# One diffusion-transformer layer on one core: output-weight factors, split attention rows, head norm per pair, routing by four tiles

## The chip, the cores and the metric

One Trainium2 core runs the whole layer as one program. The metric is the device time of one execution in microseconds; "before" is the median of three runs. The engines are PE (matrix products), DVE (VectorE), ACT (ScalarE), POOL (GpSimd) and SP (SyncE, which issues most DMAs). Each engine takes its instructions strictly in order and meets the others at semaphores.

## The reference

The layer takes 2048 latent tokens and 256 context tokens of width 1024. After adaptive norm and one input projection, half of the columns go to attention (8 query heads of 64, 2 key/value heads), half to a short gated convolution in 8 groups of 64 channels. Each head's output is RMS-normalised with its own gain, both halves are joined and projected, and the result is added with a gate. A second adaptive norm feeds a mixture of experts: one of 4 groups, then two of its 8 experts, each a SwiGLU of inner width 768.

```python
def merge_out(a, cv, attn_g, conv_g, w_out):
    return concat([head_rms(a, attn_g, 8), head_rms(cv, conv_g, 8)], axis=-1) @ w_out

x_new = x + gt1 * merge_out(ax, convx, attn_out_g, conv_out_g, w_out)
hx2 = rms_norm(x_new, norm2_g) * (1 + sc2) + sh2
x_new = x_new + gt2 * hier_moe(hx2, ...)      # top 1 of 4 groups, top 2 of 8 experts
out = rms_norm(x_new, final_g)
```

Inputs and outputs are float32. The kernel reaches that accuracy from float16 products: an operand is stored as a float16 part and the float16 remainder ("hi" and "lo"), and three products (hi by hi, hi by lo, lo by hi) take the place of one.

## The kernel before

**Stages.** First (0 to 235 us of the profile) queries, keys and values are projected, normalised, rotated and stored. The attention stage follows, to 1417 us: 32 units (four blocks of 512 queries by 8 heads, `units`), each of nine steps of two key tiles. In a step PE makes scores (`scores`, L480), ACT exponentiates them twice, as float32 and as float16, DVE or POOL subtracts the one from the other (`rest`, L494: after the convolution every other step goes to POOL), and PE multiplies with the values (`values`, L503). The softmax needs each query's maximum beforehand: `max_piece` (L456) multiplies 128 queries with up to 512 keys into one of three PSUM banks `mxp`, and DVE reduces the bank to a column. The 2304 keys are four pieces of 512 and one of 256, so a unit has 20 pieces; they run about a unit ahead of the scores.

Between these steps PE is given fillers (`fillers`, L1016): first the convolution (`conv_gen`, up to 895 us), beside it the modulation and the output weights (`out_weights`, L673), then, from 895 us, the output projection of the first twelve token tiles (`out_gen`, L975). A tail from 1417 to 1545 us does the last four tiles and the remaining routing, and begins to load expert weights. The expert stage follows.

**What the change touches.** `finish_unit` (L520) ends a unit: copy from PSUM to `ob`, squares, sum, POOL's power -1/2, product `on`; after every odd head the pair is transposed through the PSUM bank `ms` (a tag with one bank, which the maxima, the logits and the routing use too), scaled by the gain column on ACT into `oT` and stored to the DRAM tensor `mixT` as float32. `load_mix` (L748) later loads a token tile of 8 x 128 columns, and `split_mix` (L760) multiplies the convolution half by gain and reciprocal root, then makes hi and lo of both halves: in the attention stage on DVE, in the tail with the casts on ACT. `last_mix` (L770) does the last head pair, which may arrive later. `proj` (L776) makes 48 products of 512 columns per tile into PSUM, `evict` adds the residual. `logits` (L825) transposes the row, makes the second norm and the 36 router logits; `route` (L846), after every second tile, picks groups and experts with some thirty small DVE instructions and two exponentials, counts slots with small products on PE and scatters the token entries to `lists` by indirect DMAs from POOL, one for each tile and choice.

**What sets the order.** The loop from L1099 writes a step's scores, maxima, values, one filler at a pace (`fill`, L1085) and the pieces of `finish_unit`; `go_on` (L962) advances logits and routing. From this text a planner at compile time lays out the order of each engine. It may move instructions past others of the same engine; what it lays out is then fixed.

Of the kernel before, what the change touches and what calls it, by code (L numbers as in the profile page):

```python
# [9 lines left out]
F32 = mybir.dt.float32  # L10
F32R = mybir.dt.float32r
F16 = mybir.dt.float16
# [47 lines left out]
def tile_block(ctx: ExitStack, tc: tile.TileContext, x, c, ctxt, c_ctx, w_mod, b_mod, norm1_g, w_in,  # L60
# [17 lines left out]
    mixT = dram.tile([KT, P, S], F32, name="mixT")  # L78
# [59 lines left out]
    eps_l = kvp.tile([P, 1], F32, name="eps_l")  # L138


    with ExitStack() as st:
# [281 lines left out]
        V.tensor_scalar(eps_l, pb, 1024.0, None, op0=OP.mult)  # L423
        vfv = vf.rearrange("p t (g d) -> p t g d", g=2)
# [7 lines left out]
    if True:  # L432
# [23 lines left out]
        def max_piece(u, j, i):  # L456
            h = u[1]
            o, n = PIECES[i]
            if j == 0 and i == 0:
                rowmax[u] = sm.tile([P, 4, len(PIECES)], F32, name="mx")  # L460
            p_ = pp.tile([P, 512], F32, name="mxp", bufs=3)
            T.matmul(p_[:, :n], q1[u][:, j * P:(j + 1) * P], k1T[:, h // 4, o:o + n], start=True, stop=True)  # L462
            V.tensor_reduce(rowmax[u][:, j, i:i + 1], p_[:, :n], axis=AX.X, op=OP.max)  # L463
# [56 lines left out]
        def finish_unit(u):  # L520
            cq, h = u
            ob = op_.tile([P, 4, HD + 1], F32, name="ob", bufs=2)
            A.copy(ob, oraw.pop(u))  # L523
            yield
            sq = op_.tile([P, 4, HD], F32, name="osq")
            A.activation(sq, ob[:, :, 0:HD], AF.Square)
            l1 = sm.tile([P, 4], F32, name="ol1")
            V.tensor_scalar(l1, ob[:, :, HD], eps_l, None, op0=OP.mult)
            l2 = sm.tile([P, 4], F32, name="ol2")
            V.scalar_tensor_tensor(l2, l1, EPS, l1, op0=OP.mult, op1=OP.mult)  # L530
            yield
            ss = sm.tile([P, 4], F32, name="oss")
            V.tensor_reduce(ss, sq, axis=AX.X, op=OP.add)
            var = sm.tile([P, 4], F32, name="ovar")
            V.scalar_tensor_tensor(var, ss, 1.0 / HD, l2, op0=OP.mult, op1=OP.add)
            r = sm.tile([P, 4], F32, name="orr")
            G.tensor_tensor(r, var, mhalf[:, :4], op=OP.pow)
            yield
            if h % 2 == 0:
                pair[cq] = op_.tile([P, 4, 2, HD], F32, name="on", bufs=2)  # L540
            on = pair[cq]
            V.tensor_mul(on[:, :, h % 2], ob[:, :, 0:HD], r[:, :, None].to_broadcast([P, 4, HD]))
            if h % 2:
                yield
                k = h // 2
# [3 lines left out]
                oT = op_.tile([P, QC], F32, name="oT", bufs=2)  # L549
# [8 lines left out]
        def conv_gen():  # L558
# [5 lines left out]
            def finish(ct, vb, gb, n, t0, lo):  # L564
                t1 = cp.tile([P, CH], F32, name="t1", bufs=2)
                V.tensor_scalar(t1[:, :n], vb[:, 0:n], cols[:, 32 + ct:33 + ct], None, op0=OP.mult)
# [3 lines left out]
                nc.sync.dma_start(mixT[4 + ct, :, t0 + lo:t0 + n], t1[:, lo:n])  # L570
# [102 lines left out]
        def out_weights():  # L673
            g1 = mp.tile([P, D], F32, name="g1")
# [12 lines left out]
            for q, (k, n) in enumerate(todo):  # L687
# [5 lines left out]
                A.activation(woh[:, k, cs], s_, AF.Copy, scale=WS)  # L693
                V.scalar_tensor_tensor(wol[:, k, cs], s_, WS, woh[:, k, cs], op0=OP.mult, op1=OP.subtract)
# [53 lines left out]
        def load_mix(bp, tt):  # L748
            ts = slice(tt * P, (tt + 1) * P)
            mf = bp.tile([P, KT, P], F32, name="mf")  # L750
            nc.sync.dma_start(mf[:, 4:8], mixT[4:8, :, ts].rearrange("k p s -> p k s"))
            n = ready[tt] + 1
            dm["sp"] = nc.sync.dma_start(mf[:, 0:n], mixT[0:n, :, ts].rearrange("k p s -> p k s"))
# [4 lines left out]
            return mf, rb, n  # L758

        def split_mix(bp, mf, rb, after_attn):  # L760
            for k in range(4):
                V.scalar_tensor_tensor(mf[:, 4 + k], mf[:, 4 + k], cols[:, 28 + k:29 + k], rb[:, k], op0=OP.mult, op1=OP.mult)
            mh = bp.tile([P, KT, P], F16, name="mh")
            ml = bp.tile([P, KT, P], F16, name="ml")
# [3 lines left out]
            return mh, ml  # L768

        def last_mix(mf, mh, ml, tt):  # L770
            if loads[tt][2] < 4:
                dm["sp"] = nc.sync.dma_start(mf[:, 3], mixT[3, :, tt * P:(tt + 1) * P])
            V.tensor_copy(mh[:, 3], mf[:, 3])
            V.tensor_sub(ml[:, 3], mf[:, 3], mh[:, 3])

        def proj(bp, mf, mh, ml, xt, tt, banks, eng):  # L776
# [4 lines left out]
            def part(po, n, ks):  # L781
                cs = slice(n * 512, (n + 1) * 512)
                for ko, k in enumerate(ks):
                    for i, (m_, w_) in enumerate(((mh, woh), (mh, wol), (ml, woh))):
# [825 lines left out]
```

## Time and profile before

| | |
|---|---|
| Runs | 2559.11, 2562.71, 2563.91 us; median 2562.71 |
| Profiled execution | 2567.82 us, of which the span 2566.0 |
| Granted clock, mean | 0.956 |
| PE | 2317.3 us, 90% of the span |
| DVE | 2013.4 us, 78% |
| ACT | 1684.5 us, 66% |
| POOL | 673.4 us, 26% |

The span runs from the first to the last instruction of the profiled execution. In a group of instructions a row gives line, engine, operation, output and inputs with shapes, the count, the busy time of all and the mean of one, and then the idle time of the engine just ahead of them with what ended it. A wait row reads "who, at which line, waited for whom: us in total, times, longest". The granted clock is the share of TensorE's full speed of 2.4 GHz that was granted, as a mean over the stretch; its lower level is 1.2 GHz.

### The profile page before, as it was taken

The page shows a single profiled execution, that of the slowest core. Times are in us where ns is not written, and L with a number is a line of the kernel's source. Part 1 is how long each engine was busy: PE and PEld are TensorE (multiplying, and loading weights), DVE is VectorE, ACT ScalarE, POOL GpSimd, SP SyncE. Part 2 cuts the span into 40 slices and gives each one's busy share as a digit, 9 for nine tenths or more (in the row PEclk, how much of TensorE's full clock was granted, in tenths as well). Part 3 has the DMA queues.
Part 4 walks back from the last instruction along what each step waited for, and adds up shares of the span by engine and source line. Part 5 has one row for each costly group of instructions (what it writes and reads, how often), then busy time and mean ns, then how long its engine had stood idle before and what let it go on. Part 6 is the DMA issues. An engine that isn't in the chain of part 4 may idle for free. (4 is left out here: it accounts for less than half of the span.)

```text
span 2566.0 us, 64760 instructions
## 1 busy us (share of the span) xinstructions
PE 2317.3 (90%) x26923; PEld 1784.0 (70%) x26923; DVE 2013.4 (78%) x3480; ACT 1684.5 (66%) x3177; POOL 673.4 (26%) x442
## 2 busy tenths in 40 slices
PE   7998988989999988979888949999999999999964
PEld 2555765666777745545455539999899989999953
DVE  4777789898777788888887747778788887888865
ACT  4764555666666765656556427777778886888853
POOL 1331124221222234444444231121111121111122
PEclk9998999999999989999999969999999999999987
DMA  8543133341111052112211768999999999999986
GB/s 310 201 122 89 58 124 103 101 130 52 49 34 51 30 112 78 48 62 69 69 51 50 251 209 301 319 331 332 329 360 355 358 355 339 342 351 356 349 310 242
DMA packets 230215, 499.25 MB, mean 195 GB/s; under 512 B 50465, under 2 KB 97949, under 8 KB 226846
## 3 DMA queue, kind: packets, MB, share of 16 engines
q1 hardware_dynamic: 192054, 429.41, 47.8%
q0 software_dynamic: 16032, 39.85, 6.2%
q10 hardware_dynamic: 21832, 25.82, 2.9%
q8 instruction: 212, 3.47, 0.5%
q14 instruction: 85, 0.70, 0.1%
HBM read 427.20 MB, written 67.90 MB: 193 GB/s over the span
## 5 line engine op out<-in xcount | busy, mean ns | idle before, releaser
L1194 DVE SCALAR_TENSOR_TENSOR wr<-raw,wr 128x1024 f16<-128x1024 f32 x576 | 684.1, 1219 | 111.7 <-ACT wr L1192 109.5
L1192 ACT ACTIVATE wr<-raw 128x1024 f16<-128x1024 f32 x576 | 587.4, 1055 | 79.8 <-DMA raw<-in_w_down_dram 23.8
L491 ACT ACTIVATE pf<-st 128x512 f32<-128x512 f32 x576 | 345.1, 599 | 283.9 <-PE st L490 225.4
L463 DVE TENSOR_REDUCE mx<-mxp 128x1 f32<-128x512 f32 (+1 forms) x640 | 392.5, 629 | 69.4 <-PE mxp L462 68.3
L498 POOL TENSOR_TENSOR pl<-pf,ph 128x1024 f16<-128x1024 f32 x125 | 273.4, 2187 | 621.8 <-PE o L516 274.3
L1345 PEld LDWEIGHTS <-wr 128*128 128x128 f16 x4032 | 396.8, 98 | 20.5 <-issue 17.5
L1346 PEld LDWEIGHTS <-wr 128*128 128x128 f16 x4032 | 396.3, 98 | 13.2 <-issue 8.6
L1344 PEld LDWEIGHTS <-wr 128*128 128x128 f16 x4032 | 396.4, 98 | 4.2 <-issue 0.9
L492 ACT ACTIVATE ph<-st 128x512 f16<-128x512 f32 x576 | 344.6, 598 | 0.0
L1344 PE MATMUL pu<-x,wr 128*128 128x152 f16 (+19 forms) x1536 | 295.8, 227 | 8.1 <-DVE sg L1361 7.7
L1344 PE MATMUL pg<-x,wr 128*128 128x152 f16 (+19 forms) x1536 | 295.0, 226 | 3.3 <-ACT sg L1359 2.9
L1346 PE MATMUL pg<-x,wr 128*128 128x152 f16 (+19 forms) x1536 | 294.5, 226 | 3.6 <-DVE wr L1194 3.5
L1345 PE MATMUL pu<-x,wr 128*128 128x152 f16 (+19 forms) x1536 | 295.6, 227 | 0.0
L1346 PE MATMUL pu<-x,wr 128*128 128x152 f16 (+19 forms) x1536 | 295.4, 227 | 0.0
L1345 PE MATMUL pg<-x,wr 128*128 128x152 f16 (+19 forms) x1536 | 294.6, 226 | 0.0
L615 PE MATMUL z<-h,cwh 128*128 128x256 f16 x1536 | 275.8, 275 | 9.9 <-DVE vb L623 6.4
L462 PE MATMUL mxp<-k1T,q 128*128 128x512 f16 (+1 forms) x640 | 231.5, 365 | 38.5 <-DVE mx L463 37.1
L516 PE MATMUL o<-vh,pl 128*128 128x65 f16 x2304 | 246.8, 196 | 7.1 <-DVE pl L500 4.6
L514 PE MATMUL o<-vh,ph 128*128 128x65 f16 x2304 | 247.7, 197 | 0.3 <-ACT ob L523 0.2
L515 PE MATMUL o<-vlo,ph 128*128 128x64 f16 x2304 | 247.4, 195 | 0.0
L489 PE MATMUL st<-q,k1T 128*128 128x512 f16 x576 | 222.2, 386 | 16.1 <-ACT ph L492 15.5
L514 PEld LDWEIGHTS <-ph 128*128 128x128 f16 x2304 | 218.0, 100 | 22.1 <-issue 6.6
(363 smaller groups left out, 5414.2 us busy)
## 6 DMA issues: line engine op xcount, KB each, us to landing
raw<-in_w_down_dram SPq DMA_DIRECT2D x64, 1536.0 KB
raw<-in_w_gate_dram SPq DMA_DIRECT2D x63, 1536.0 KB
raw<-in_w_up_dram SPq DMA_DIRECT2D x63, 1536.0 KB
xt<-in_x_dram SPq DMA_DIRECT2D x32, 512.0 KB
wmod<-in_w_mod_dram SPq DMA_DIRECT2D x64, 256.0 KB
h<-hs SPq DMA_DIRECT2D x16, 1024.0 KB
w<-in_w_mod_dram SPq DMA_DIRECT2D x16, 512.0 KB
hs<-h ACTq DMA_DIRECT2D x8, 1024.0 KB
```

The source lines that it names most:

```text
L463: V.tensor_reduce(rowmax[u][:, j, i:i + 1], p_[:, :n], axis=AX.X, op=OP.max)
L491: A.activation(pf[:, i], p_, AF.Exp)
L492: A.activation(ph[:, i], p_, AF.Exp)
L498: G.tensor_tensor(pl, pf, ph, op=OP.subtract)
L514: T.matmul(po[:, j], ph[:, i, js], vh1[:, k, g], start=f, stop=False, skip_group_check=True)
L515: T.matmul(po[:, j, 0:HD], ph[:, i, js], vlo[:, k, g], start=False, stop=False, skip_group_check=True)
L615: T.matmul(z, w_[:, k, cs], h[:, a_, k, :], start=(n == 0), stop=(n == 3 * KT - 1))
L1192: A.activation(w[:, 0, sl], t[:, sl], AF.Copy, scale=WS)
L1194: V.scalar_tensor_tensor(w[:, 1, sl], t[:, sl], WS, w[:, 0, sl], op0=OP.mult, op1=OP.subtract)
L1344: T.matmul(p_[:, :C], w_[:, 0, kk, cs], x[:, 0, k, :C], start=first, stop=False)
L1345: T.matmul(p_[:, :C], w_[:, 0, kk, cs], x[:, 1, k, :C], start=False, stop=False)
L1346: T.matmul(p_[:, :C], w_[:, 1, kk, cs], x[:, 0, k, :C], start=False, stop=last)
```

## The change

- The gains of both halves (attention and convolution) leave the rows and go into the output weights: `out_weights` scales by a column `wg` = gain x 256 instead of 256.
- `finish_unit` copies both heads of a pair into one tile and does squares, sums, root and product once per pair. The square of the softmax sums with its epsilon moves from two DVE instructions to one on ACT (`eps_q`). After the transpose ACT makes the hi part from PSUM, DVE the lo part, and two DMAs store them to `mixA`, laid out by token tile in pieces of 256 bytes.
- `load_mix` loads the convolution half as float32 and the attention half as the two parts, straight into the tile that `proj` reads. `split_mix` is left with one product of 512 columns, a cast on ACT and one subtraction, all for the convolution half; `last_mix` with a load.
- `route` handles four tiles at once for the first twelve tiles, two for the last four. Its tiles are twice as wide; a four-tile call makes eight scatters.
- The 256-key pieces of two query blocks share a bank and one reduction: 18 pieces per unit instead of 20.
- The first product of the convolution's three taps moves from DVE to ACT.

```diff
+            if h % 2:
+                sq = op_.tile([P, 8, HD], F32, name="osq")
+                A.activation(sq.rearrange("p (h j) d -> p h j d", h=2), ob[:, :, :, 0:HD], AF.Square)
+                A.activation(l2, ob.rearrange("p h j d -> p (h j) d")[:, :, HD], AF.Square, scale=eps_q)
...
+                V.tensor_reduce(ss, sq, axis=AX.X, op=OP.add)
+                V.scalar_tensor_tensor(var, ss, 1.0 / HD, l2, op0=OP.mult, op1=OP.add)
+                G.tensor_tensor(r, var, mhalf[:, :8], op=OP.pow)
+                V.tensor_tensor(on.rearrange("p j h d -> p h j d"), ob[:, :, :, 0:HD], ...)
...
-                A.activation(oT, tq, AF.Copy, scale=cols[:, 24 + k:25 + k])
-                nc.sync.dma_start(mixT[k, :, cq * QC:(cq + 1) * QC], oT)
+                A.copy(oT[:, 0], tq)
+                V.tensor_sub(oT[:, 1], tq, oT[:, 0])
+                for a in range(2):
+                    nc.sync.dma_start(mixA[cq * 4:(cq + 1) * 4, :, a, k].rearrange("j p s -> p j s"),
+                                      oT[:, a].rearrange("p (j s) -> p j s", j=4))
...
-                V.tensor_scalar(t1[:, :n], vb[:, 0:n], cols[:, 32 + ct:33 + ct], None, op0=OP.mult)
+                A.activation(t1[:, :n], vb[:, 0:n], AF.Copy, scale=cols[:, 32 + ct:33 + ct])
...
+            for a, j in enumerate(js):
+                T.matmul(p_[:, a * n:(a + 1) * n], q1[u][:, j * P:(j + 1) * P], k1T[:, h // 4, o:o + n], start=True, stop=True)
+            V.tensor_reduce(rowmax[u][:, js[0]:js[-1] + 1, i:i + 1], p_[:, :len(js) * n].rearrange("p (a n) -> p a n", a=len(js)),
+                            axis=AX.X, op=OP.max)
...
-            mf = bp.tile([P, KT, P], F32, name="mf")
-            nc.sync.dma_start(mf[:, 4:8], mixT[4:8, :, ts].rearrange("k p s -> p k s"))
-            n = ready[tt] + 1
-            dm["sp"] = nc.sync.dma_start(mf[:, 0:n], mixT[0:n, :, ts].rearrange("k p s -> p k s"))
+            mf = bp.tile([P, 4, P], F32, name="mf")
+            dm["sp"] = nc.sync.dma_start(mf, mixT[:, :, ts].rearrange("k p s -> p k s"))
...
+            m = bp.tile([P, 2, KT, P], F16, name="mh")
+            n = ready[tt] + 1
+            dm["sp"] = nc.sync.dma_start(m[:, :, 0:n], mixA[tt, :, :, 0:n])
...
-            for k in range(4):
-                V.scalar_tensor_tensor(mf[:, 4 + k], mf[:, 4 + k], cols[:, 28 + k:29 + k], rb[:, k], op0=OP.mult, op1=OP.mult)
-            for ks in (slice(4, 8), slice(0, 3)):
-                (A.copy if after_attn else V.tensor_copy)(mh[:, ks], mf[:, ks])
-                V.tensor_sub(ml[:, ks], mf[:, ks], mh[:, ks])
+            V.tensor_mul(mf, mf, rb)
+            A.copy(m[:, 0, 4:8], mf)
+            V.tensor_sub(m[:, 1, 4:8], mf, m[:, 0, 4:8])
...
-            V.tensor_copy(mh[:, 3], mf[:, 3])
-            V.tensor_sub(ml[:, 3], mf[:, 3], mh[:, 3])
...
+            n2 = 4 if tt < NT - 4 else 2
...
-            for i in range(4):
+            for i in range(2 * n2):
                 w_ = G.indirect_dma_start(out=lists[:, :], ...)
...
-                if tt % 2:
-                    after.append([route(tt - 1), None])
+                if tt % 2 and tt >= NT - 4:
+                    after.append([route(tt - 1, 2), None])
+                elif tt % 4 == 3:
+                    after.append([route(tt - 3, 4), None])
```

## Rows read from the trace of the kernel before

**Rows 1.** Windows by stage: from:to, length; busy PE, PEld, DVE, ACT, POOL; clock; DMA
```profile
390.00:642.00 252.00, 232.60 (x2677) 162.82 (x2676) 225.88 (x393) 160.47 (x336) 66.75 (x37) 0.98 0.31 96
642.00:895.00 253.00, 252.35 (x3072) 184.10 (x3070) 193.47 (x366) 172.35 (x353) 61.11 (x32) 1.00 0.12 39
895.00:1417.00 522.00, 450.44 (x4757) 274.00 (x4756) 427.27 (x797) 311.94 (x631) 231.13 (x128) 0.92 0.25 69
1545.00:2438.00 893.00, 872.97 (x12167) 827.61 (x12165) 734.34 (x974) 703.41 (x1196) 157.72 (x94) 1.00 0.99 343
```

**Rows 2.** PE's waits, 895 to 1417: us in total, times, longest
```profile
PE mxp L462 <- DVE mx L463: 35.0, 20, 4.7
PE st L489 <- ACT ph L492: 7.9, 19, 1.1
...
PE o L516 <- POOL pl L498: 2.4, 3, 1.0
```

**Rows 3.** DVE's waits, 895 to 1417, same columns
```profile
DVE mf L762 <- DMA mf<-mixT: 15.3, 6, 3.7
DVE h L820 <- POOL n2r L118: 12.9, 5, 5.4
DVE on L542 <- POOL orr L537: 10.8, 10, 2.6
```

**Rows 4.** DVE instruction groups, 895 to 1417: busy us, mean ns; idle before
```profile
L463 DVE TENSOR_REDUCE mx<-mxp 128x1 f32<-128x512 f32 x205 | 136.2, 681 | 16.2 <-PE mxp L462 15.8
...
L463 DVE TENSOR_REDUCE mx<-mxp 128x1 f32<-128x256 f32 x52 | 21.4, 412 | 5.5 <-PE mxp L462 5.5
L762 DVE SCALAR_TENSOR_TENSOR mf<-mf,cols,rb 128x128 f32<-128x128 f32 x56 | 21.2, 422 | 20.4 <-DMA mf<-mixT 15.3 <-DMA rb<-cvrs 3.1 <-issue 2.0
L542 DVE TENSOR_TENSOR on<-ob,orr 128x256 f32<-128x256 f32 x14 | 18.9, 1352 | 10.8 <-POOL orr L537 10.8
L767 DVE TENSOR_TENSOR ml<-mf,mh 128x512 f16<-128x512 f32 x13 | 15.5, 1195 | 0.0
...
L767 DVE TENSOR_TENSOR ml<-mf,mh 128x384 f16<-128x384 f32 x13 | 11.4, 879 | 0.0
L766 DVE CAST mh<-mf 128x512 f16<-128x512 f32 x12 | 10.6, 886 | 0.2 <-PE z L785 0.2
L773 DVE CAST mh<-mf 128x128 f16<-128x128 f32 x12 | 10.5, 877 | 0.0
L774 DVE TENSOR_TENSOR ml<-mf,mh 128x128 f16<-128x128 f32 x12 | 10.3, 862 | 0.0
L766 DVE CAST mh<-mf 128x384 f16<-128x384 f32 x12 | 7.5, 626 | 1.0 <-DMA mf<-mixT 1.0
L528 DVE TENSOR_SCALAR ol<-ob,eps_l 128x4 f32<-128x4 f32 x14 | 7.5, 534 | 0.0
...
L902 DVE TENSOR_TENSOR ee<-ee,pen 128x64 f32<-128x64 f32 x5 | 5.0, 990 | 2.1 <-ACT ee L861 2.1
...
L931 DVE TENSOR_TENSOR en<-en,m 128x2 f32<-128x2 f32 x5 | 0.8, 150 | 0.0
```

**Rows 5.** DVE instruction groups of the tail, 1417 to 1545
```profile
L767 DVE TENSOR_TENSOR ml<-mf,mh 128x512 f16<-128x512 f32 x3 | 2.1, 684 | 0.0
L767 DVE TENSOR_TENSOR ml<-mf,mh 128x384 f16<-128x384 f32 x3 | 1.7, 551 | 0.0
...
L773 DVE CAST mh<-mf 128x128 f16<-128x128 f32 x4 | 0.9, 222 | 5.4 <-PE z L785 5.4
...
L902 DVE TENSOR_TENSOR ee<-ee,pen 128x64 f32<-128x64 f32 x3 | 0.7, 221 | 0.6 <-ACT ee L861 0.6
```

**Rows 6.** POOL in order of time: start us, us, line
```profile
1052.21 1.19 POOL L946 DMA_INDIRECT lists<-en,di  x1 [0.33 <-DVE ss L814]
...
1058.33 2.13 POOL L498 TENSOR_TENSOR pl<-pf,ph 128x1024 f16<-128x1024 f32 x1
```

**Rows 7.** ACT instruction group, 895 to 1417
```profile
L793 ACT ACTIVATE sq<-xt 128x512 bf16<-128x512 f32 x22 | 13.9, 631 | 18.6 <-DVE xt L791 18.5
```

More of the change, by code (lines that the diff above doesn't have):

```diff
@@ L138, in tile_block @@
     eps_l = kvp.tile([P, 1], F32, name="eps_l")
+    eps_q = kvp.tile([P, 1], F32, name="eps_q")
     with ExitStack() as st:
@@ L521, in finish_unit @@
             cq, h = u
-            ob = op_.tile([P, 4, HD + 1], F32, name="ob", bufs=2)
-            A.copy(ob, oraw.pop(u))
+            if h % 2 == 0:
+                pair[cq] = op_.tile([P, 2, 4, HD + 1], F32, name="ob", bufs=2)
+            ob = pair[cq]
+            A.copy(ob[:, h % 2], oraw.pop(u))
             yield
[L525 to L537, printed above, removed]
@@ L840, in logits, with route, new @@
                 T.matmul(pl[:, 0:NG + NE], hT[:, k, :], wr[:, k, :], start=(k == 0), stop=(k == KT - 1))
-            V.scalar_tensor_tensor(dm["L2"][:, tt % 2], pl[:, 0:NG + NE], r, dm["cB"], op0=OP.mult, op1=OP.add)
+            V.scalar_tensor_tensor(dm["L2"][:, tt % n2], pl[:, 0:NG + NE], r, dm["cB"], op0=OP.mult, op1=OP.add)
             yield
             dm["sp"] = nc.sync.dma_start(h2d[tt * P:(tt + 1) * P, :], h2)
-        def route(tt):
+        def route(tt, n2):
             sp, L = dm["p"], dm["L2"]
+            def new(shape, dt, name, axis=1, per=1):
+                full = list(shape)
+                full[axis] = 4 * per
+                return sp.tile(full, dt, name=name)[(slice(None),) * axis + (slice(0, n2 * per),)]
             def over(src, n, op, tag):
-                m = sp.tile([P, 2], F32, name=tag)
+                m = new([P, n2], F32, tag)
                 V.tensor_reduce(m, src, axis=AX.X, op=op)
@@ L869, in idx @@
             def idx(n):
-                return iota64[:, None, :n].to_broadcast([P, 2, n])
+                return iota64[:, None, :n].to_broadcast([P, n2, n])
             def below(e, n, tag, top=None):
-                cd = sp.tile([P, 2, n], F32, name=tag)
+                cd = new([P, n2, n], F32, tag)
                 if top is None:
@@ L890, in route @@
             yield
-            Lm = sp.tile([P, 2, NE], F32, name="Lm")
+            Lm = new([P, n2, NE], F32, "Lm")
             def groups(t):
@@ L911, in route @@
             yield
-            both = sp.tile([P, 2, NE], BF, name="both")
+            both = new([P, n2, NE], BF, "both")
             V.tensor_add(both, OH[:, 0], OH[:, 1])
@@ L917, in route @@
             pr = pp.tile([P, 512], F32, name="ms")
-            for i in range(2):
+            for i in range(n2):
                 o_ = pr[:, i * NE:(i + 1) * NE]
                 T.matmul(o_, upper, both[:, i], start=True, stop=False)
-                if i:
-                    T.matmul(o_, ones_b, both[:, 0], start=False, stop=False)
+                for b in range(i):
+                    T.matmul(o_, ones_b, both[:, b], start=False, stop=False)
                 T.matmul(o_, ones_b, prior, start=False, stop=True)
-            en = sp.tile([P, 2, 2, 2], I32, name="en")
-            V.tensor_copy(en[:, :, :, 0], tokid[:, None, tt:tt + 2].to_broadcast([P, 2, 2]))
-            den = sp.tile([P, 2], F32, name="den")
+            en = new([P, 2, n2, 2], I32, "en", 2, 1)
+            V.tensor_copy(en[:, :, :, 0], tokid[:, None, tt:tt + n2].to_broadcast([P, 2, n2]))
+            den = new([P, n2], F32, "den")
             V.scalar_tensor_tensor(den, m2, 1.0, gs, op0=OP.add, op1=OP.mult)
@@ L1031, in tile_block @@
         NU = len(units)
-        NPM = len(PIECES) * 4
+        order = [(js, i) for b in (0, 2) for js, i in
+                 ([((j,), i) for j in (b, b + 1) for i in range(len(PIECES) - 1)] + [((b, b + 1), len(PIECES) - 1)])]
+        NPM = len(order)
         ND = NKT // 2
         steps = [(u, d) for u in units for d in range(ND)]
-        pieces = [(u, j, i) for u in units for j in range(4) for i in range(len(PIECES))]
+        pieces = [(u, *o) for u in units for o in order]
         tail = []
```

101 lines of the change are left out of this document (52 added, 49 removed).

## The prediction

> **What bounds the kernel now.** I read the page first: PE is busy 90% of the span, so the question is where the other tenth lies. The view of the chain that ended last is no help here (it stops after one microsecond at the final loop), so I went to the busy times by stage. The expert stage, 1545 to 2438, has PE at 873 of 893 us and the granted clock at 1.00 [rows 1]; the change touches nothing in it. The attention stage falls in two. From 642 to 895, with the convolution as filler, PE is busy 252.35 of 253 us: nothing can be won there but PE work, and the change takes none away. From 895 to 1417, with the output projection, the second norm and the routing as filler, PE is busy only 450.4 of 522 us at a clock of 0.92, and DVE 427 us [rows 1]. This stage is where the time can come from: 71.6 us of idle PE, and a clock that falls (between its levels of 2.4 and 1.2 GHz) where PE has idled. PE work at full clock is about 450.4 x 0.92 = 414 us, an estimate, so the clock costs 522 - 71.6 - 414 = 36 us.
>
> Then the waits of PE in that stage: 35.0 us of the 71.6 are 20 waits of the maximum pass for a free PSUM bank, which DVE's reduction has to empty; ACT's exponentials cause 7.9 us and POOL's subtractions 2.4 [rows 2]. So DVE is the engine that is late. It is late for two reasons. It has 427 us to do, and, working in order, it also stands still with the reductions behind it: 15.3 us for the load of the mixed tile, 12.9 for POOL's reciprocal root of the second norm, 10.8 for that of the head norm [rows 3]. Busy and held together are 466 of 522 us, 89%. For scale: at 642 to 895 DVE is busy 76% and PE idles 0.3%; at 390 to 642 it is busy 90% and PE idles 19.4 of 252 us, 7.7% [rows 1].
>
> **The change, part by part, in the stage 895 to 1417** (DVE time; each term has a low end, where only the undisturbed price is saved, and a high end at this stage's own prices).
>
> The attention half of the mixed tile arrives already split, so four groups go: 11.4 + 7.5 + 10.5 + 10.3 = 39.7 us [rows 4]. Much of this is waiting inside the instruction: the cast of 128 columns means 877 ns here and 222 ns in the tail, where POOL does no subtractions [rows 4, 5]. The low end is 12 x 0.222 = 2.7 for it, 13 x 0.551 = 7.2 for the 384-column subtraction [rows 5], and a quarter, the same ratio, of the other two: 14.4 in all.
>
> The convolution half: its cast goes to ACT (10.6 us; low end, a quarter, 2.7). 56 products of 128 columns, 21.2 us, become 14 of 512. The trace has no such product; the nearest row is the 512-column subtraction, 0.684 us undisturbed and 1.195 here [rows 4, 5], so 9.6 to 16.7 us come back and 4.5 to 11.6 are saved.
>
> The head norm per pair: the small scaling of the softmax sums goes to ACT (7.5 us; low end 1.9); its follower and the shorter count of reductions I cost at nothing, since the pair's reductions are twice as wide. 14 products, 18.9 us, become 7 of twice the width, each between 0.684 and twice 1.352 us, so 0 to 14.1 is saved. New are 7 subtractions from PSUM, 512 columns, at the 0.681 of the reduction of that shape: 4.8 us [rows 4, 5]. Together -2.9 to 16.8.
>
> Paired maxima: 52 reductions of 256 columns, 21.4 us, become 26 of 512 at 0.681, 17.7 [rows 4]: 3.7 saved, certain.
>
> Routing: 32 groups of small instructions, the dearest and the cheapest of them in [rows 4], come to 53.2 us for the five routes that fall in this stage, 10.6 each. Two routes of four tiles take their place, the third falls into the tail as one of two tiles does now. A wider one costs perhaps 12: some 17 groups get 64 columns more, at (684 - 551)/128 = 1.04 ns a column [rows 5] 1.1 us, and two more additions. High end 53.2 - 24 = 29.2. At the undisturbed ratio of the dearest, 221 to 990 ns [rows 4, 5], a route would be 2.4 and a wider one 3.9: low end 4.
>
> Sum: 26 to 112 us. I take 80, nearer to the stage's own prices, because fewer exposed instructions meet POOL less often. DVE then does 347 us and is held 34 (the head-norm wait halves): 381, under PE's 414. PE becomes the engine that sets the stage. DVE's share of a stage of 460 us would be 76% busy, 83% with the holds, between the two stages above. I expect the waits for maxima to fall from 35 to 12 us and the other 36.6 us of idle to halve: 30 left, and a clock loss in proportion, 36 x 30/71.6 = 15. 414 + 30 + 15 = 459, a gain of 63.
>
> **Elsewhere and against.** 390 to 642: DVE loses one pass of the convolution to ACT and pairs maxima; the stage has 19.4 us of PE idle and 2% of clock, 24 at most [rows 1]. I take a third: gain 8 (0 to 24). ACT's added pass there is hidden by ACT being busy only 160 of 252 us. From 642 to 895 nothing, with PE full. The two filler steps that two fewer pieces take from the opening move later by about a step and cost nothing; the folded output weights cost nothing, being the same instructions with a column as factor.
>
> Scatters: POOL issues them in a block. Four, and a short root behind them, now hold it from 1052.2 until the subtraction starts at 1058.3 [rows 6]; eight hold it some 5 us longer, with the roots of the norms and the subtractions queued behind, and PE and DVE waiting for those. Twice in the stage, 0 to 10 us; PE waits only 2.4 for POOL now [rows 2], so I take 4.
>
> PSUM bank: the transposed pair now frees its bank only after DVE's subtraction, so transposes and logits behind it wait for DVE's queue. 7 pairs here, from nothing to the longest hold of DVE, 5.4 us [rows 3]: 0 to 38; 2, since that bank's next user mostly comes a step later.
>
> ACT: the copy of the convolution half stands in ACT's order behind DVE's product, and the exponentials stand behind it. The nearest row is the square of the evicted tile, which waits for DVE in the same way: 18.6 us for 22, 0.85 each [rows 7]; 12 copies hold ACT 10 us, of which PE, with two score banks, sees little: 2 (0 to 79, see the rivals).
>
> Tail, 1417 to 1545: four tiles lose casts and subtractions (up to 4 us off), the last pair's chain grows by wider steps and the new subtraction (about 2), its store becomes two, of smaller pieces, and the route of tiles 8 to 11 brings eight scatters, 5 us longer. -4 to +12; I take +4.
>
> Sum: -63 - 8 + 4 + 2 + 2 + 4 = -59. The profiled execution took 2567.8 us (span 2566.0), so it would become 2509; the median of the runs is 5.1 us lower, so 2504 against 2562.7. About 0.2%, 5 us, is what a measurement of this kernel can tell from no change.
>
> **Rivals.** First, the waits move instead of vanishing. The 222 ns that become 877 [rows 4, 5] are time in which POOL works; its subtractions stay, and the next DVE instruction pays. Then DVE saves the low end, 26: 401 busy and 34 held, 435, and at today's 89% the stage takes 487, a gain of 35; with the other terms (-8 + 12) 2532. For it: POOL's busy time, 231 us [rows 1], hardly changes. Against: the reductions from PSUM, 681 here as in every stage, do not pay, and they are a third of DVE. This is what the Trainium skill says (SBUF — State Buffer, Terms: the port pair that DVE and GpSimd share is held for a whole instruction and the loser is blocked entirely); the two means agree with it, and by it alone the first rival would be the forecast.
>
> Second, PE alone sets the stage, as at 642 to 895: the idle goes but for 15 us, clock loss to 7: 436, a gain of 86, and 16 at 390 to 642; with 2 against, 2463. For it that stage; against it the chains through DVE, POOL and DMA, which the convolution lacks.
>
> Third, slower: ACT is held. Each of 12 copies waits for a product that waits for the tile's load (up to 3.7 us) in a queue that may stand for the norm's root (up to 5.4) [rows 3]. At both, 9.1 us, less 2.5 of cover (four exponentials of about 0.63 on two banks, priced by the 512-column pass of [rows 7]), PE loses 12 x 6.6 = 79, and the time is 2504 - 2 + 79 = 2581. It decides from a hold of 2.5 + 61/12 = 7.6 us per copy. Against it the 0.85 of the like instruction.
>
> Fourth, the order on each engine, which a planner lays out anew, gives the stage new waits as long as the old: 2563.
>
> **How the numbers follow.** Forecast 0.52, the waits move 0.22, PE alone 0.14, ACT held 0.08, no change 0.04. The forecast's own range is 2484 to 2527. The range reaches to the second rival and past the first, 2462 to 2545; outside lie the slower case, about 0.06 below and 0.04 above. Faster 0.87, same 0.05, slower 0.08.
>
> **What would show it.** Right: 895 to 1417 shrinks to about 460 us, clock 0.96 or more, PE's waits for maxima under 15 us, DVE near 350. First rival: the means of the remaining DVE instructions with two SBUF operands grow. Second: PE idle under 20 in the stage. Third: exponentials waiting for the product of the mixed tile, PE for exponentials far over 7.9 us. Wrong altogether: the stage unchanged although DVE's busy time fell, or a tail over 140 us.

## The result, and the profile after

The changed kernel takes 2540.4 us (median of 4 runs, 2537.8 to 2544.1) against 2560.9 of the kernel before in the same session: a ratio of 0.9911, 95% interval 0.9897 to 0.9924. By the medians it is faster by 20.5 us (the interval of the ratio stands for some 20 to 26); the forecast was 59. The direction was right and the size was not. The profiled execution took 2540.7 us (span 2538.9), 27.2 less than the profiled one of before, which lay 5 above the median given for it.

In the spans, 27.1 us apart, the gain can be dated by ACT's copies of the 32 finished attention units. Up to the 18th: 903.5 us before, 904.7 after (+1.2). The 14 units behind it: 513.9 before, 487.5 after (-26.4). From the last unit to the first transpose of the expert stage: 100.0 and 104.6 (+4.6). The expert stage: 1048.6 and 1042.1 (-6.5). So the attention stage with the output projection gave nearly all of it, and gave half of what it should.

The stages of the changed kernel, as in [rows 1] (from:to, length; busy PE, PEld, DVE, ACT, POOL; clock; DMA):

```profile
395.00:647.00 252.00, 233.86 (x2709) 163.74 (x2709) 223.10 (x345) 166.62 (x350) 64.22 (x32) 0.97 0.31 94
647.00:900.00 253.00, 252.03 (x3070) 183.93 (x3068) 193.24 (x309) 178.35 (x368) 55.93 (x27) 1.00 0.13 39
900.00:1392.00 492.00, 433.57 (x4708) 266.70 (x4706) 365.64 (x532) 312.55 (x629) 220.23 (x115) 0.94 0.27 74
1524.00:2411.00 887.00, 870.46 (x12153) 825.51 (x12152) 732.59 (x971) 703.19 (x1197) 164.00 (x94) 1.00 0.99 344
```

In the third line DVE lost 62 us (80 were forecast), but PE still idles 58.4 us where 30 were forecast, and its clock is 0.94 where 0.96 or more was forecast. What PE waits for there, answering [rows 2]:

```profile
PE mxp L466 <- DVE mx L467: 23.4, 9, 6.5
PE ms L838 <- DVE mr L478: 12.7, 2, 9.2
PE st L494 <- ACT ph L497: 12.0, 16, 4.7
...
PE o L521 <- POOL pl L503: 1.3, 3, 0.5
```

The waits for maxima fell from 20 to 9, but their longest grew from 4.7 to 6.5 us, and a wait that the kernel before did not have in this size stands second: 12.7 us in two pieces, one of 9.2. DVE's own waits, answering [rows 3], name the source: its wait for the root of the second norm did not shrink like the other two of [rows 3]; it grew, and its longest went from 5.4 to 7.0.

```profile
DVE h L824 <- POOL n2r L119: 15.9, 4, 7.0
...
DVE on L547 <- POOL orr L544: 6.7, 5, 1.8
...
DVE mf L771 <- DMA mf<-mixT: 4.5, 1, 4.5
```

The long wait read through three engines in order of time. POOL first (start us, us, line; in brackets idle before): eight scatters in a row, 1.27 us apart, and only then the root.

```profile
1127.97 1.19 POOL L957 DMA_INDIRECT lists<-en,di  x1 [2.25 <-DVE ss L818]
1129.47 1.06 POOL L957 DMA_INDIRECT lists<-en,di  x1 [0.31 <-issue]
...
1137.15 0.96 POOL L957 DMA_INDIRECT lists<-en,di  x1 [0.30 <-issue]
1138.13 0.58 POOL L119 TENSOR_TENSOR n2r<-n2v,mhalf 128x1 f32<-128x1 f32 x1
```

DVE had made the root's input at 1128.25, stood 6.47 us for the root, and kept the second half of a maximum's row (L478) behind it:

```profile
1128.25 0.14 DVE L117 TENSOR_SCALAR n2v<-ss 128x1 f32<-128x1 f32 x1
...
1132.00 0.27 DVE L477 TENSOR_SCALAR mr<-ms 4x128 f16<-4x128 f32 x1
1138.74 3.15 DVE L824 SCALAR_TENSOR_TENSOR h<-xt,n2r,A 128x1024 f32<-128x1024 f32 x1 [6.47 <-POOL n2r L119]
1141.82 0.27 DVE L478 SCALAR_TENSOR_TENSOR mr<-ms,mr 4x128 f16<-4x128 f32 x1
```

And PE, whose next transposes need the one bank that L478 still reads, stood from 1132.9 on:

```profile
1132.73 0.19 PE L520 MATMUL o<-vlo,ph 128*128 128x64 f16 x1
1142.14 1.11 PE L838 MATMUL ms<-ident,xt 128*128 128x128 f32 x4 [9.22 <-DVE mr L478]
```

The second block of eight, from 1292 to 1302, does the same to the maxima (6.50 us until 1306.91), and behind it the clock is at the lower of its levels:

```profile
1306.91 0.58 PE L466 MATMUL mxp<-k1T,q 128*128 128x512 f16 x1 [6.50 <-DVE mx L467]
1306.00:1314.00 8.00, 7.09 (x47) 5.75 (x47) 6.06 (x9) 1.26 (x3) 2.40 (x2) 0.50 0.38 133
```

One group of DVE besides grew while the work around it went (900 to 1392; busy us, mean ns | idle before). The addition of one column took 243 ns before (L814, the first line) and takes 1405 now (L818). The product of 512 columns costs 1.42 us, nearly as much as the four products that it replaced, 21.2 us for 14 tiles or 1.5 each [rows 4].

```profile
L814 DVE TENSOR_TENSOR ss<-ss 128x1 f32<-128x1 f32 x11 | 2.7, 243 | 0.0
L771 DVE TENSOR_TENSOR mf<-mf,rb 128x512 f32<-128x512 f32 x15 | 21.3, 1422 | 10.4 <-DMA rb<-cvrs 5.9 <-DMA mf<-mixT 4.5
L818 DVE TENSOR_TENSOR ss<-ss 128x1 f32<-128x1 f32 x11 | 15.5, 1405 | 0.3
...
L773 DVE TENSOR_TENSOR mh<-mf,mh 128x512 f16<-128x512 f32 x13 | 12.8, 984 | 0.9 <-ACT mh L772 0.9
L547 DVE TENSOR_TENSOR on<-ob,orr 128x512 f32<-128x512 f32 x7 | 8.6, 1230 | 6.7 <-POOL orr L544 6.7
L542 DVE SCALAR_TENSOR_TENSOR ovar<-oss,ol 128x8 f32<-128x8 f32 x7 | 6.5, 935 | 0.3
```

These means mix two kinds, and the trace shows what the long ones have in common: each ends just behind an instruction of POOL. Of the eleven additions eight take 1.5 to 2.0 us and end within 0.03 us of the end of a POOL subtraction; the other three take 0.15. Of the fifteen products eight take 1.0 to 2.9 us and end 0.54 to 0.56 us behind POOL, seven of them behind its addition of the second norm (L825) and one behind a subtraction; the other seven take 0.67 to 0.69. One of each, with the instruction of POOL beside it:

```profile
1374.91 2.57 POOL L503 TENSOR_TENSOR pl<-pf,ph 128x1024 f16<-128x1024 f32 x1 [3.66 <-ACT mh L772]
1375.52 1.97 DVE L818 TENSOR_TENSOR ss<-ss 128x1 f32<-128x1 f32 x1
1379.71 3.27 POOL L825 TENSOR_TENSOR h<-h,B 128x1024 f32<-128x1024 f32 x1 [1.40 <-DVE h L824]
1380.68 2.85 DVE L771 TENSOR_TENSOR mf<-mf,rb 128x512 f32<-128x512 f32 x1
```

### The profile page after: what moved, and what is told of

The parts are those of the page before. It is cut to its first block, busy times and chain, and to the rows that moved or that the text cites. A ratio compares the mean times of both kernels' runs of the same rounds, so it can differ in the third digit from the quotient of the medians.

```text
span 2538.9 us, 64496 instructions
## 1 busy us (share of the span) xinstructions
PE 2306.7 (91%) x26935; PEld 1779.2 (70%) x26935; DVE 1946.5 (77%) x3074; ACT 1702.9 (67%) x3215; POOL 661.8 (26%) x425
## 5 line engine op out<-in xcount | busy, mean ns | idle before, releaser
L467 DVE TENSOR_REDUCE mx<-mxp 128x1 f32<-128x512 f32 (+1 forms) x576 | 383.2, 682 | 77.1 <-PE mxp L466 75.3
L505 DVE TENSOR_TENSOR pl<-pf,ph 128x1024 f16<-128x1024 f32 x164 | 210.3, 1282 | 50.9 <-PE o L521 34.3
L466 PE MATMUL mxp<-k1T,q 128*128 128x512 f16 (+1 forms) x640 | 220.5, 364 | 24.7 <-DVE mx L467 24.3
```

The costliest lines, as they stand in the source:

```text
L467: V.tensor_reduce(rowmax[u][:, js[0]:js[-1] + 1, i:i + 1], p_[:, :len(js) * n].rearrange("p (a n) -> p a n", a=len(js)), axis=AX.X, op=OP.max)
```

## The experiments

Theory A: the blocks of eight scatters hold POOL, POOL's late root holds DVE, and DVE holds PE. Rivals: B, DVE's saving was mis-sized because its waits moved to other instructions; C, the PSUM bank (`ms`) that the transposed pair now holds longer. Times are compared by their ratio to the kernel before, which ran beside them each time.

**1. Scatters one at a time.** One scatter per filler step of the next tile, each behind a subtraction of POOL; the route in the tail keeps its block.

```diff
-            for i in range(2 * n2):
+            def put1(i):
                 w_ = G.indirect_dma_start(out=lists[:, :],
...
+            for i in range(2 * n2):
+                if tt < NT - 8:
+                    puts.append((put1, i))
+                else:
+                    put1(i)
...
+                    if puts:
+                        f, i = puts.pop(0)
+                        with tc.issue_after(dm["pl"].ins):
+                            f(i)
                     yield
```

> Theory A: the blocks of eight scatters on POOL (10.1 us each, 1128.0 to 1138.1 and 1292 to 1302) keep POOL from the reciprocal root of the second norm; DVE, in order, stands behind the product that needs the root, and PE behind DVE. One scatter per filler step, each behind a subtraction, takes that away: the two attention units that hold the blocks (46.4 and 41.0 us) go to about 33, the two waits of PE over 6 us (9.22 and 6.50) are gone, the idle clock with them; 2516 to 2524 us, 16 to 24 under the changed kernel. Rival B: the blocks cost little (what they hold would be waited for otherwise), the saving of DVE was mis-sized and its waits moved: 2535 to 2541. Against both: sixteen issues among the subtractions could delay every exponential's partner: slower than 2545.

2520.5 us, ratio 0.9837 (0.9817 to 0.9857): 20 us under the changed kernel. The two units that hold the blocks (the 25th and the 30th; the expectation named the 29th, of 41.0 us, in place of the 30th, of 40.8), first in the changed kernel, then here, as windows:

```profile
1111.50:1157.90 46.40, 34.42 (x357) 21.46 (x356) 31.24 (x58) 23.16 (x49) 23.34 (x16) 0.85 0.24 62
1287.40:1328.30 40.90, 34.14 (x335) 21.38 (x334) 25.82 (x37) 20.85 (x42) 21.29 (x15) 0.83 0.22 52
```

```profile
1110.70:1150.10 39.40, 34.34 (x357) 20.70 (x354) 31.91 (x57) 23.13 (x48) 25.32 (x16) 0.91 0.29 73
1279.40:1310.80 31.40, 29.51 (x335) 18.51 (x334) 26.56 (x37) 20.77 (x41) 24.35 (x15) 1.00 0.22 65
```

The same 357 and 335 matmuls take 7.0 and 9.5 us less: PE idles 6.9 and 4.9 us less, and is busy 4.7 less at a better clock. Those 16.5 are most of the 18.2 by which the 14 units got shorter (487.5 to 469.3). The two longest waits of PE are gone. Theory A holds, at the size expected.

**2. The root ahead of the block.** The eight scatters stay together, behind the root of the second norm.

```diff
-        G.tensor_tensor(r, var, mhalf[:, :n], op=OP.pow)
+        root[0] = G.tensor_tensor(r, var, mhalf[:, :n], op=OP.pow)
...
+                while puts:
+                    f, i = puts.pop(0)
+                    with tc.issue_after(root[0].ins):
+                        f(i)
```

> The eight scatters stay one block but stand behind the tile's root of the second norm in POOL's order, so the root is no longer late and only the subtractions behind the block are. If the harm goes through the root (theory A): 2518 to 2526, DVE's waits for the root fall from 15.9 us to under 6. If it goes through the late subtractions, the low halves of the weights: 2534 to 2541, and PE waits for POOL's subtractions in place of the second norm, over 6 us in one piece. Rival B: 2535 to 2541 with neither.

2535.5 us, 0.9897 (0.9879 to 0.9915): a quarter of the gain at best. The root is no longer late (DVE waits 3.0 us for it), but the block now holds what stands behind it, POOL's subtractions, and with them PE, and DVE's next entries wait until the scatters have read the old ones. PE's wait, then DVE's (895 to 1400; us in total, times, longest):

```profile
PE o L523 <- POOL pl L505: 10.3, 4, 5.5
```

```profile
DVE en L939 <- DMA lists<-en,di: 14.3, 2, 7.7
```

So theory A holds for the block and not for the root: it is not the root's place in the queue that costs. DVE, served with the root, stands 6.56 and 7.73 us for the table of entries that the same scatters still read, where the late root held it 6.47 and 6.96, and PE stands behind POOL's subtractions besides. The block costs by its ten microseconds; how much comes by which of these two waits, this run does not separate.

**3. All but the routing by four tiles.** The split store, the head norm by pairs, the weights, the tap and the paired maxima stay; shown against the changed kernel.

```diff
-            n2 = 4 if tt < NT - 4 else 2
...
-                if tt % 2 and tt >= NT - 4:
-                    after.append([route(tt - 1, 2), None])
-                elif tt % 4 == 3:
-                    after.append([route(tt - 3, 4), None])
+                if tt % 2:
+                    after.append([route(tt - 1), None])
```

> All of the change but the routing by four tiles, so blocks of four scatters as in the kernel before. Theory A: routing by four gave DVE some 25 us and lost two holds of about 10 us; without it the time is 2535 to 2545, near the changed kernel's 2540, and no unit stands out by more than 8 us. Rival B: DVE's busy time is what sets this stage, the routing's part of the DVE saving is lost and nothing comes back: 2548 to 2556.

2551.9 us, 0.9961 (0.9947 to 0.9975). Of the 20.5 us the routing brings 11, net of its blocks; beside the run with single scatters it brings some 31. The rest of the change brings 10. The expectation of B came out here, but experiment 1 shows that the blocks take back two thirds of what the routing gives, so A and B are both at work. The 31 may be too much: the kernel of this run still issues its scatters in blocks of four, which cost time in the changed kernel (experiment 12), and routing by two tiles with single scatters was not tried on it.

**4. The bank freed early.** ACT copies the transposed pair out of PSUM first; both halves come from that copy.

```diff
-                A.copy(oT[:, 0], tq)
-                V.tensor_sub(oT[:, 1], tq, oT[:, 0])
+                of = op_.tile([P, QC], F32, name="of")
+                A.copy(of, tq)
+                A.copy(oT[:, 0], of)
+                V.tensor_sub(oT[:, 1], of, oT[:, 0])
```

> ACT copies the transposed pair out of PSUM to float32 first, so the one bank that the transposes, the sums of squares and the logits share is free after one copy; both halves are made from SBUF after that. Theory C: the longer hold of that bank by DVE's subtraction is a part of the lost gain: PE's waits for it (2.6 us for the subtraction by name, some of 12.7 and 2.7) go, 2530 to 2536. Theories A and B: no one waits long for it; 14 more ACT copies of 256 columns, about 0.5 us each, cost nothing to 4: 2538 to 2545.

2538.4 us, 0.9913 (0.9895 to 0.9932) against 0.9911: no difference. PE's waits behind the subtraction (2.6 us) go, and nothing follows. Theory C falls. The added copies are of 512 columns and 7 in the stage, 0.6 us each, not 14 of 256 as the expectation has it.

**5. Single scatters and two buffers for their entries.**

```diff
-                return sp.tile(full, dt, name=name)[(slice(None),) * axis + (slice(0, n2 * per),)]
+                return sp.tile(full, dt, name=name, bufs=2 if name == "en" else None)[(slice(None),) * axis + (slice(0, n2 * per),)]
```

> The spread scatters, and the table of entries that the scatters read in two buffers in place of one. In the run with spread scatters DVE stands 8.8 and 2.7 us in the tail (1415 to 1424 and 1455 to 1458) until scatters of the route before have read that table; PE then idles 6.7 us for the residual addition behind it. If that wait is on the path that sets the end: 2510 to 2515, the tail from the last attention unit to the first expert transpose about 95 us in place of 104. If another chain through the tail (PE's projection of the last four tiles, the last two tiles' logits) sets it anyway: 2517 to 2523.

2520.0 us, 0.9833: as in experiment 1. The second of DVE's two waits in the tail went, the first did not (9.0 us until 1422.5), and PE still idles 6.8 us behind it. Why a second buffer does not lift that wait was not found; whether it would pay stays open.

**6. A quarter of POOL's subtraction, with single scatters.** The kernel leaves out three quarters of the low halves that POOL makes, so it prices POOL's work and is no version to use.

```diff
-                dm["pl"] = G.tensor_tensor(pl, pf, ph, op=OP.subtract)
+                dm["pl"] = G.tensor_tensor(pl[:, :, 0:P], pf[:, :, 0:P], ph[:, :, 0:P], op=OP.subtract)
+                part.add((u, d))
...
-                    T.matmul(po[:, j], pl[:, i, js], vh1[:, k, g], start=False, stop=l, skip_group_check=True)
+                    T.matmul(po[:, j], (ph if j and (u, d) in part else pl)[:, i, js], vh1[:, k, g], start=False, stop=l, skip_group_check=True)
```

> The spread scatters, but POOL makes only a quarter of each of its low halves (128 of 512 columns of each half), and the value matmuls take the high half in place of the other three quarters: same PE and ACT work, part of the low correction left out. The moved waits: DVE's instructions with operands in SBUF cost 41 us more between 895 and 1375 than the same shapes cost in the tail (the 128x1 addition 1.41 us against 0.16, eleven times). If POOL's large subtractions hold them: that excess falls to 8 to 15 us, DVE is 25 to 33 us less busy, and the time falls to 2506 to 2515. If something else makes them slow: excess over 30 us, time 2517 to 2524.

2479.9 us, 0.968 (0.9664 to 0.9696): 40 us under the run with whole subtractions, where 5 to 14 were expected. The 14 units with single scatters, then with the quarter:

```profile
905.50:1374.80 469.30, 423.99 (x4644) 259.21 (x4643) 361.46 (x523) 308.59 (x619) 223.82 (x115) 0.96 0.27 76
```

```profile
887.60:1330.10 442.50, 415.48 (x4643) 258.79 (x4642) 311.25 (x523) 308.13 (x619) 122.10 (x114) 0.97 0.27 80
```

The same 523 instructions of DVE take 50 us less, and PE's idle falls from 45 to 27 us. The excess over the tail's prices (for each shape that occurs in both, the mean here less the mean in the tail, times the count) falls from 41.1 to 3.7 us, and the addition of one column is cheap again:

```profile
L819 DVE TENSOR_TENSOR ss<-ss 128x1 f32<-128x1 f32 x11 | 2.9, 263 | 0.4 <-ACT sq L798 0.3
```

So POOL's subtraction is what most of this excess waits for, inside the busy time of DVE's instructions, as the ends in the trace of the changed kernel say too. The Trainium skill (SBUF — State Buffer, Terms) says that DVE and GpSimd take turns at a shared pair of ports, held for a whole instruction, with the loser blocked; the fall from 41.1 to 3.7 agrees. The expectation was too small twice: it left out the nine units from 310 to 648, which lose 18 us too (338.0 to 319.9), and DVE's own large subtractions, which the tail does not have (56 in this stretch, 1473 to 1235 ns). Not all of the 40 us need come through DVE: in the 14 units ACT's waits for POOL's subtraction fall as well, from 20.5 to 3.8 us, and no run separates the two.

**7. The tap back on DVE.**

```diff
-                A.activation(t1[:, :n], vb[:, 0:n], AF.Copy, scale=cols[:, 32 + ct:33 + ct])
+                V.tensor_scalar(t1[:, :n], vb[:, 0:n], cols[:, 32 + ct:33 + ct], None, op0=OP.mult)
```

> The changed kernel with the convolution's first tap back on DVE. The prediction's term for 390 to 642 (8 us of gain): if the tap on ACT and the paired maxima gave anything there, putting the tap back costs 3 to 8 us: 2543 to 2548, and the sixth to ninth attention unit longer by that. If this stretch was set by PE and by the loads of the convolution's weights: 2537 to 2543.

2540.6 us, 0.9912: nothing. The tenth unit ends at 645.8 us, against 646.9 with the tap on ACT.

**8. As 3, without the paired maxima.**

```diff
-            for a, j in enumerate(js):
-                T.matmul(p_[:, a * n:(a + 1) * n], q1[u][:, j * P:(j + 1) * P], k1T[:, h // 4, o:o + n], start=True, stop=True)
+            T.matmul(p_[:, :n], q1[u][:, j * P:(j + 1) * P], k1T[:, h // 4, o:o + n], start=True, stop=True)
...
```

> As the run without four-tile routing (2551.9), and with maxima of one 256-column piece each in place of two: the split store, the head norm by pairs, the weights and the tap alone. If the pairing only saves 3.7 us of DVE as forecast: 2552 to 2557. If a pair of pieces in one bank costs PE as much in banks that come free later, the two cancel: 2548 to 2552. If the pairing carries the gain by fewer waits for a bank: over 2558.

2548.9 us, 0.9942 (0.9926 to 0.9959) against 0.9961 (0.9947 to 0.9975): the pairing gains nothing that shows. Attention ends at 1397.8 us in both; the stretch up to the 18th unit is 14 us shorter with the pairs (901.4 against 915.8), the 14 units behind it 14 longer (496.4 against 482.0).

**9. The kernel before with single scatters.** The edit of experiment 1 for the blocks of four.

```diff
...
+            for i in range(4):
+                if tt < NT - 6:
+                    puts.append((put1, i))
+                else:
+                    put1(i)
...
```

> The kernel before, with the four scatters of each of its first five routes issued one per filler step behind a subtraction, as the eight were. Whether the 20 us that spreading gave are a cost that the change added (four to eight in a block) or one that the kernel before had too: if a block costs by its length and four are mostly hidden, this gains 0 to 4: 2558 to 2563. If each scatter in a block costs the same, twenty scatters against sixteen bring the same 20 us: 2540 to 2548.

2573.3 us against 2567.6 beside it, 1.002 (1.0001 to 1.0038): no gain, though DVE's wait for that root falls from 12.9 us [rows 3] to 2.1 (902 to 1419). The cost that single scatters take away came with the change.

```profile
DVE h L820 <- POOL n2r L118: 2.1, 2, 1.7
```

**10. The kernel before with a quarter of the subtraction.** The edit of experiment 6.

```diff
-                G.tensor_tensor(pl, pf, ph, op=OP.subtract)
+                G.tensor_tensor(pl[:, :, 0:P], pf[:, :, 0:P], ph[:, :, 0:P], op=OP.subtract)
+                part.add((u, d))
...
```

> The kernel before, with POOL making a quarter of each of its low halves and the value matmuls taking the high half for the rest (part of the low correction left out). DVE's excess over the prices of the tail is 69.5 us between 895 and 1417 here and 41 in the kernel with spread scatters, where the same cut brought 40 us. If the change earned its time mostly by having fewer instructions that POOL can hold: this falls by 50 to 65, to 2497 to 2512, and the two kernels without most of POOL's work lie only 17 to 32 us apart (2480 for the other), less than the 42 that they lie apart with it. If it earned it by DVE's work itself: a fall of 35 to 45, 2517 to 2527.

2496.2 us, 0.9723 (0.9695 to 0.9752): 71 us, more than the 50 to 65 expected. The 14 units of the kernel before, then of this one:

```profile
903.50:1417.40 513.90, 442.59 (x4641) 269.41 (x4640) 419.75 (x784) 304.05 (x613) 226.05 (x126) 0.92 0.24 67
```

```profile
892.90:1347.80 454.90, 419.30 (x4639) 257.31 (x4637) 353.19 (x783) 303.57 (x613) 126.36 (x125) 0.97 0.27 74
```

Without most of POOL's work the two kernels lie 0.0043 apart (0.9723 to 0.968), 11 us; with it, and with single scatters, 0.0163, 42 us. So about three quarters of what the change can give go when POOL's work goes. That fits a gain from fewer instructions for POOL to hold, but it does not show it: with POOL's holds gone, DVE is less late in both kernels, and then less work of DVE counts for less too. Nor is the 11 sharp, since the intervals of the two ratios (0.9695 to 0.9752 and 0.9664 to 0.9696) touch.

**11. The sum of the second norm on POOL, with single scatters.**

```diff
-            V.tensor_add(ss[:, 2:3], ss[:, 0:1], ss[:, 1:2])
-            r = rstd_of(bp, ss[:, 2:3], 1, 1.0 / D, "n2")
+            G.tensor_tensor(ss[:, 2:3], ss[:, 0:1], ss[:, 1:2], op=OP.add)
+            r = rstd_of(bp, ss[:, 2:3], 1, 1.0 / D, "n2", G)
```

> The spread scatters, and the 128x1 addition and scaling of the second norm's sums of squares on POOL, right before its root, in place of DVE. The addition cost DVE 15.5 us in the stage, 13.8 of them over its price in the tail. If that is a wait that simply moves to the next DVE instruction: the excess over the tail stays at 35 to 42 us and the time at 2517 to 2523. If it goes with the instruction: DVE is 13 to 16 us less busy, excess 26 to 29, and 2508 to 2516.

2531.5 us, 0.9869 (0.9838 to 0.9901) against 0.9837 (0.9817 to 0.9857): not faster, perhaps slower. DVE's busy time fell by 16 us (361.5 to 345.4) and its excess to 27.5, as the second branch had it, and the time did not follow. DVE's wait for the root, here, then in experiment 1 (895 to 1385):

```profile
DVE h L824 <- POOL n2r L119: 11.9, 5, 3.1
```

```profile
DVE h L824 <- POOL n2r L119: 2.5, 2, 1.8
```

The sum now waits in POOL's queue, and DVE waits for the root: 9.4 of the 16 us are back as idle time, and PE's waits for maxima are 26.1 us in place of 17.0. Most of the hold moved from busy to idle time.

**12 and 13. Two blocks of four, beside single scatters again.**

```diff
-                if tt < NT - 8:
+                if tt < NT - 8 and i >= n2:
                     puts.append((put1, i))
...
-                    if puts:
+                    while puts and n == 9:
```

> The changed kernel with each block of eight scatters cut into two of four: the first four stay where they are, ahead of the root of the second norm, the other four come three subtractions later. If a block costs by its length, half stays: four ahead of the root still hold it some 5 us, 2526 to 2534. If a block of four is hidden (spreading the fours of the kernel before gained nothing) and only what is beyond it costs: 2516 to 2524, as with single scatters.

> The single scatters once more, beside the two blocks of four on one chip and in more rounds: 0.982 to 0.986 of the kernel before. The run with two blocks of four is judged against it: within 5 us, or 6 to 14 us above.

Single scatters: 2522.7 us in five runs, 0.9833 (0.9816 to 0.9851), the fastest version that leaves nothing out, and ahead of both kernels. Two blocks: 2535.1 us, 0.9888 (0.9872 to 0.9904), 12 above. Cutting the block in two takes off a third of its cost or less; four in a block are not hidden in the changed kernel. The 25th and 30th units with two blocks:

```profile
1114.40:1157.20 42.80, 35.22 (x356) 21.56 (x355) 31.38 (x57) 23.11 (x49) 20.45 (x13) 0.88 0.22 68
1286.50:1325.20 38.70, 34.02 (x335) 21.32 (x334) 24.56 (x34) 20.78 (x42) 19.50 (x14) 0.87 0.21 53
```

In the 30th PE waits 3.31 us once for a maximum (until 1304.05), and the clock goes to 0.87 where it was 1.00 without that wait.

```profile
1304.05 0.58 PE L466 MATMUL mxp<-k1T,q 128*128 128x512 f16 x1 [3.31 <-DVE mx L467]
```

That four cost nothing in the kernel before (experiment 9) and cost here is not explained by a run; there DVE is busy 422 of 517 us and has other holds that come as late, but this was only read, not tried.

## Why the prediction was wrong

The forecast missed by 36 us. Two of its steps failed: the price of the scatters, and the DVE time that it took as removed where POOL's holds only moved to other instructions, in two stretches. By its own steps, in the profiled executions:

- **The scatters: the path was wrong.** It saw them, with the right queue behind them, and let eight hold POOL some 5 us longer than four. Twice in the stage it allowed 0 to 10 us and took 4. Single scatters brought 18 in the 14 units and 20 in the whole. The price of the block itself was right (10.1 us for eight, against 6.1 for four with a root [rows 6]); wrong was to charge PE by what it then waited for POOL, 2.4 us [rows 2]. The wait came through DVE, under the names of the maxima and of the norm's bank, and each of the two long ones left PE at a low clock besides (0.75 from 1142 to 1150, 0.50 from 1306 to 1314). Missed by 14.
- **DVE in the attention stage: the term was too large.** The forecast took 80 "because fewer exposed instructions meet POOL less often". It was 62 us less, 58.5 in the same 14 units, not 80. Gone as forecast: the attention half's four groups, the scaling of the softmax sums, the maxima (21.4 to 17.8), the routing. Not gone: the 512-column product took 21.3 us where 9.6 to 16.7 was the bound, the one-column addition grew by 12.8 us and the variance (L542) by 3.3; the long ones of all three end behind an instruction of POOL. With single scatters the 14 units take 469.3 us, 44.6 less than before, where 59 were forecast without the scatters: missed by 14. PE idles 45 us there, not 30.
- **390 to 642: the same error.** A gain of 8 was forecast and none came: +1.2 up to the 18th unit, and neither the tap (experiment 7) nor the pairs (experiment 8) move the time. DVE saved hardly anything there, 223.10 us busy from 395 to 647 against 225.88 from 390 to 642 [rows 1]. The first tap left DVE (4.6 us for 10), but the other two grew (before, then after):

```profile
L567 DVE SCALAR_TENSOR_TENSOR t<-vb,cols,t 128x256 f32<-128x256 f32 x10 | 4.8, 477 | 0.0
L568 DVE SCALAR_TENSOR_TENSOR t<-vb,cols,t 128x256 f32<-128x256 f32 x10 | 6.6, 655 | 0.1
L574 DVE SCALAR_TENSOR_TENSOR t<-vb,cols,t 128x256 f32<-128x256 f32 x11 | 10.5, 957 | 1.1 <-ACT t L573 1.0
L575 DVE SCALAR_TENSOR_TENSOR t<-vb,cols,t 128x256 f32<-128x256 f32 x11 | 9.6, 875 | 0.1
```

  Of these 22 now seven take 0.9 to 2.4 us and end 0.28 us behind an instruction of POOL (four behind a subtraction, three behind its product L701 for the output weights); the others take 0.47 or 0.48. With a quarter of the subtraction (experiment 6) the two means are 555 and 602 ns, and the nine units around them lose 18 us. Missed by 9.
- **The bank (2), ACT's copies (2), the tail (+4).** Near: experiment 4 shows the first at nothing, and the tail grew by 4.6. ACT's copies were not tried alone; PE's waits for exponentials grew by 4 us.
- **The expert stage, and the median.** 6.5 us came from the expert stage, where nothing was forecast. It took 1039 to 1047 us in the profiles of the changed kernel and its variants and 1048 to 1052 in the three of the kernel before and its variants; what makes the difference was not tried. The 5 us between the profiled execution and the median, taken off the forecast, were not there after.

Together 14 + 14 + 9 - 6.5 + 5 + 0.6: the 36.

Of the rivals, the first came nearest (2532), and its mechanism is real: the waits did move, to the one-column addition, the variance, the 512-column product and the two taps, and experiments 6 and 10 give the size of POOL's holds, 50 and 67 us of DVE in this stage. The misses of 14 and 9 are laid to it; that is read from the traces and fits experiment 6, but no run took these holds alone away. It is not the whole, and its 2532 was near for another reason too: DVE saved 62 and not 26, and the blocks, which it priced as the forecast did, took 20. The second, PE alone, is what experiment 6 approaches with 27 us of idle. The third did not decide: ACT waited for the product only twice, 9.9 us in all. The fourth, no gain, is outside the interval.

## What to carry to other kernels

A scatter that POOL issues occupies POOL in order, here 1.27 us from one to the next: count a block by its length, look at what is queued behind it on that engine, and follow the wait through the next engine too, for it shows under other names. Here it paid to issue them one at a time among the engine's own work (20 us); moving a short operation ahead of the block won 5 and mostly changed who waits. And busy time of DVE beside a busy POOL is part work and part waiting: compare each shape with a stretch where POOL rests before it is taken as work, and do not count such time as won by moving the instruction to the engine that it waits for.

## What was not expected of the hardware

- Three quarters less of POOL's subtraction took 67 us from DVE's busy time in the kernel before (419.75 to 353.19) and 50 in the one with single scatters: that is nearly as much as the 80 that the whole change was to save there.
- The product of 512 columns with both operands in SBUF took from 0.67 to 2.85 us (mean 1.42), and it did not become faster with a quarter of POOL's subtraction (mean 1.36), unlike the other instructions. The trace of experiment 6 says why: seven of its fifteen products there take 1.0 to 2.7 us, and all seven end 0.55 or 0.56 us behind POOL's addition of the second norm (128x1024), which that edit left whole. The first of them:

```profile
957.89 2.35 POOL L826 TENSOR_TENSOR h<-h,B 128x1024 f32<-128x1024 f32 x1 [1.16 <-DVE h L825]
958.34 2.47 DVE L772 TENSOR_TENSOR mf<-mf,rb 128x512 f32<-128x512 f32 x1
```

  No run moved or shortened that addition.
